# RWKV tail: outputs of the first eight heads issued between the readings of the second eight, whose banks are of the other tag

## The chip, the cores and the metric

The kernel runs on one core of one Trainium2 chip. The metric is the device time of one execution in microseconds, given as the median over several runs.

## The reference

A decoder trunk of four layers, 256 positions of width 1024, in float32. Layers 0 and 3 mix positions with RWKV-7, layer 1 with Mamba-2, layer 2 with windowed attention; each mixer stands between two half-step SwiGLU blocks, and each sub-layer is normed and shifted, scaled and gated by a vector that comes from the condition `c` through `ada_w`. The change is in the RWKV-7 mixer, and there behind the recurrence:

```
state = state * w_t + sa * (kk_t * a_t) + v_t * k_t      # per head, 64 x 64
y_t   = state @ r_t                                      # the reading
y     = (y - mean) * rsqrt(var + RW_GN_EPS) * ln_w + ln_b
bonus = sum(rh * kh * r_k) * vh
out   = ((y + bonus) * g) @ w_o
x     = x + gate * out
```

There are 16 heads of 64 channels. The sums that the norm needs run over the 64 channels of a head at each position.

## The kernel before, in words

Channels lie on the 128 partitions (two heads in a tile of 128), positions along the free axis. A tile of 128 channels and 256 positions is numbered j = 0 to 7. The 16 heads are worked in two groups g of four tiles, `jj` = 0 to 3 within the group, and the sequence in four chunks c of 64 positions.

Products with large weights take three fp32r matmuls for one in float32: weight and input are each split into a high and a low part. `unit` (L293) loads one weight tile of 512 KB on SyncE's queue into a `raw` tile, copies the high part `whi` on ScalarE (L299) and subtracts the low part `wlo` on VectorE (L303). Four `raw` tiles exist, and the modulation uses them too: `mod_step` (L247) loads one row block of `ada_w` into a `raw` tile (L252) and multiplies and sums it against `c` on VectorE (L253), with a small step behind it (L257, L261). `mod_some(n, upto)` puts n such steps into the program at that place. Of `whi` and `wlo` there are three each in the mixer.

PSUM has eight banks of 512 words, handed out by `bank(tag)` (L321): four under the tag `mm`, four under `aux`.

The program is written in one order, and a planner then sets the order of each engine's own instructions: it walks through a model of the chip's time, takes whatever is ready first, and where several are ready the one that stands earlier in the program. So an engine's order in the trace isn't the order of the source. `issue_after(ins)` forces what is traced within it behind `ins` on that engine.

Dense products can be put on a queue in pieces, each of three matmuls: `dense_queue` (L346) does so for the projections to r, k and v, and `out_proj` (L509) for the output projection, where each tile `jj` of a finished output gives eight pieces, one for each output tile of `x`, into four `mm` banks (two tiles to a bank). `fill(n)` (L370) issues the next n pieces, held behind the last product of the mixer while `hold` is set; `drain(left)` issues until `left` entries are on the queue. In the RWKV mixer `out_proj` is made with `slow=True` and `last=1`: `feed` (within it) loads the weight and puts the pieces of tile k on the queue; with the eighth tile it drains the queue, and then adds the eighth tile's products and updates `x`.

The tail of the mixer in program order, from L1552 (phase `core`):

- the chains of both groups (L1363), a step of one and a step of the other, with a `fill` and at some steps a `mod_some(1)` between. Group 0 is read within its chain by `read(0, c)` (L1402), chunk by chunk: the products go to an `mm` bank, ScalarE copies them to `ys` (L1412) and squares them (L1414), and a product with a two-column matrix of ones sums the squares into `sns`, an `mm` bank that holds 16 columns for each group.
- the last of r's queued pieces are drained.
- `bonus(4..7)` (L1336): sums on PE (L1593) into an `aux` bank, a product on VectorE (L1340), and one `mod_some(1)` each. The `fill(3)` here finds an empty queue.
- `norm(0)`, which is `rows8` (L1165): variance (L1168), reciprocal root on VectorE in 12 small steps (`rsqrt`, L573), two transposes on PE into an `aux` bank, and the split of the rows into `yth` (ScalarE, L835) and `ytl` (VectorE, L836).
- `read_heads(1, jj)` (L1419) for four tiles: the same readings for group 1, tile by tile, in an `mm` bank, with sums into the other 16 columns of `sns`, and `mod_some(2)` each.
- `outputs(0)` (L1441) for four tiles: row product `heads` (L839, products at L844) into an `aux` bank, scale and shift on VectorE (L1449, L1450), the gate's two products (`sg` and `hm`, recorded at L1077) into an `aux` bank, the gate on VectorE (L1454), the split (L318, L319), `mod_some(2)`, and `feed`.
- `norm(1)`, then `outputs(1)` in the same way; the last `feed` drains the queue.

Where a helper records the products of the mixer, all have L1077 (transposes L1081); they are told apart by their tiles. GpSimd has no part in the tail.

Of the kernel before, what the change touches and what calls it, by code (L numbers as in the profile page):

```python
# [15 lines left out]
ALU = mybir.AluOpType  # L16
# [5 lines left out]
S = 256  # L22
# [161 lines left out]
class Trunk:  # L184
# [884 lines left out]
    def rw(self, i, k):  # L1069
# [21 lines left out]
        with ExitStack() as ctx:  # L1091
# [51 lines left out]
            def lora(n, t=None):  # L1143
                return self.lora(k, n, t)
# [256 lines left out]

            def read(g, c):  # L1402

                s, uv, mr, ys, sn = ss[g], uvs[g], mrs[g], yss[g], sns[:, 16 * g : 16 * g + 16]
                o = self.bank("mm", S)
                at = slice(c * 64, c * 64 + 64)
                for jj in range(4):
                    for par, p in enumerate(half):
                        mm(hd(o, jj, p), uv[:, par, jj, c], mr[:, par, 4 * jj + c], start=True, stop=c == 0)
                    for p in half if c else ():  # L1410
                        mm(hd(o, jj, p), s[c - 1][p, jj], er[g][p, jj, c, 1:], start=False, stop=True)
                act.copy(ys[:, :, at], c64(o))  # L1412
                sq = sp.tile([P, S], F32, tag="sq", name="sq")
                act.activation(sq, o, AF.Square)  # L1414
                for jj in range(4):
                    mm(sn[half[c % 2], c // 2 * 8 + 2 * jj : c // 2 * 8 + 2 * jj + 2], sq[:, jj * 64 : jj * 64 + 64],
                       self.c("b2"), start=True, stop=True)

            def read_heads(g, jj):  # L1419

                s, uv, mr, ys, sn = ss[g], uvs[g], mrs[g], yss[g], sns[:, 16 * g : 16 * g + 16]
                o = self.bank("mm", S)
                for c in range(4):
                    at = slice(c * 64, c * 64 + 64)
                    for par, p in enumerate(half):
                        mm(o[p, at], uv[:, par, jj, c], mr[:, par, 4 * jj + c], start=True, stop=c == 0)
                    for p in half if c else ():
                        mm(o[p, at], s[c - 1][p, jj], er[g][p, jj, c, 1:], start=False, stop=True)
                act.copy(ys[:, jj], o)
                sq = sp.tile([P, S], F32, tag="sq", name="sq")  # L1430
                act.activation(sq, o, AF.Square)
                for b in range(2):
                    mm(sn[:, b * 8 + 2 * jj : b * 8 + 2 * jj + 2], sq[:, b * P : b * P + P], self.c("b2"),
                       start=True, stop=True)
# [116 lines left out]
                merge(g, *inv)  # L1551
            self.phase(f"rw{i}.core")  # L1552
            bns = slot("bn", [3, 4, P], "bn")
            sns = self.bank("mm", 32)
            hold[0] = True
            more = inner(1, bd)
            for n, _ in enumerate(one_by_one(chain(0), chain(1))):
# [4 lines left out]
                if n in (17, 20, 22):  # L1562
                    self.drain(3 - (17, 20, 22).index(n))
                    next(more)
            norm = lambda g: rows8(sns[:, 16 * g : 16 * g + 16], (ALU.mult, ALU.add), 1.0 / 64, GN_EPS)
            for jj in range(4):
                if jj >= len((17, 20, 22)):
                    self.drain(3 - jj)
                    next(more)
                self.fill(3)  # L1570
            g2, mid = lora(5), lora(4)
            for jj in range(4):
                bonus(4 + jj)
                self.mod_some(1, ahead)
                self.fill(3)
            yt = norm(0)
            yss[1] = slot("f1", [4, S], "ys")
            for jj in range(4):
                read_heads(1, jj)
                self.mod_some(2, ahead)  # L1580
                self.fill(3)
            hold[0] = False
            for _ in outputs(0, yt, g2, mid):
                pass
            for _ in outputs(1, norm(1), g2, mid):
                pass
            self.last = None

# [33 lines left out]
```

## Time and profile before

| | |
|---|---|
| median of 3 runs | 2522.41 us (2514.05 to 2526.98) |
| the profiled execution's own time | 2529.85 us |
| its span | 2527.9 us |
| granted TensorE clock, mean | 0.962 |
| TensorE busy | 2403.7 us (95%) |
| VectorE busy | 1984.8 us (79%) |
| ScalarE busy | 1262.2 us (50%) |
| tail of layer 0, from the end of the first group's sums to the last drained piece | 438.5 to 506.4 us |
| tail of layer 3, likewise | 2264.3 to 2329.9 us |

A row of the timeline gives the start in us, the duration in us, engine, line, operation, what it writes and reads, the count, and in brackets the engine's idle time ahead of it and what ended it. PE is TensorE, DVE VectorE, ACT ScalarE, SPq SyncE's DMA queue. A busy PE is not a PE at full rate: the granted clock (1.00 is full) stands in the table by stretch.

### The profile page before, as it was taken

What the parts mean: (1) busy time and instruction counts of PE and PEld (TensorE: products, weight loads), DVE (VectorE), ACT (ScalarE), POOL (GpSimd) and SP (SyncE); (2) the same over time, 40 slices, a digit from 0 to 9 for tenths busy, and PEclk for the clock granted to TensorE, in tenths of its full rate; (3) what the DMA queues carried; (4) which work ended last, traced back from release to release, by engine and by line L of the source; (5) the groups of instructions that cost most, each with busy time, mean ns of one, the idle gap of its engine ahead of it and who ended that gap; (6) DMA issues with size and microseconds to landing.
All of it is one profiled execution on the core that took longest, in us unless ns stands there. A gap on an engine that the chain in (4) does not pass through costs nothing.

```text
span 2527.9 us, 51852 instructions
## 1 busy us (share of the span) xinstructions
PE 2403.7 (95%) x20868; PEld 2247.2 (89%) x20868; DVE 1984.8 (79%) x4181; ACT 1262.2 (50%) x2261; POOL 8.1 (0%) x14
## 2 busy tenths in 40 slices
PE   6999999989999989999999999899999999998999
PEld 5998877789999988999999999799999977777999
DVE  7777687887788788988878878987788767867754
ACT  3445663254454466765445446554444465623543
POOL 0000000000000000000000000000000000000000
PEclk9999898699999999999999999989999999987999
DMA  8874224668858834455885884468758732255653
GB/s 304 288 262 167 92 94 158 234 202 291 274 196 287 285 128 135 152 178 198 302 282 188 294 286 166 151 213 293 257 180 299 263 119 72 81 174 195 211 189 117
DMA packets 145392, 521.98 MB, mean 206 GB/s; under 512 B 16128, under 2 KB 19456, under 8 KB 145024
## 3 DMA queue, kind: packets, MB, share of 16 engines
q1 hardware_dynamic: 145152, 518.67, 60.3%
q8 instruction: 164, 2.69, 0.4%
q14 instruction: 76, 0.62, 0.1%
HBM read 516.50 MB, written 2.10 MB: 205 GB/s over the span
## 4 chain that ended last, share of the span: by engine, by line
PE 52%; DMA 20%; DVE 18%; ACT 5%; issue 5%; DVEq 0%; ACTq 0%; SPq 0%
DMA raw<-ffn 11%; PE aux L1077 8%; DMA ada<-ada_w 7%; DVE wlo L303 7%; PE aux L330 5%; PE aux L328 5%; PE aux L329 5%; PE mm L328 5%; PE mm L329 4%; PE mm L330 4%; PE mm L521 3%; DVE ada L253 3%; PE mm L520 3%; PE mm L522 3%; ACT whi L299 3%
## 5 line engine op out<-in xcount | busy, mean ns | idle before, releaser
L299 ACT CAST whi<-raw 128x1024 fp32r<-128x1024 f32 x671 | 699.9, 1049 | 696.1 <-DMA raw<-ffn 476.6
L303 DVE TENSOR_TENSOR wlo<-raw,whi 128x1024 fp32r<-128x1024 f32 x671 | 816.0, 1221 | 244.0 <-ACT whi L299 240.8
L328 PE MATMUL aux<-hh,whi 128*128 128x256 f32 x2576 | 723.7, 281 | 18.6 <-DVE ft L676 16.0
L330 PE MATMUL aux<-hh,wlo 128*128 128x256 f32 x2576 | 722.1, 281 | 12.7 <-DVE wlo L303 12.4
L329 PE MATMUL aux<-hl,whi 128*128 128x256 f32 x2576 | 720.3, 280 | 0.0
L328 PEld LDWEIGHTS aux<-hh,whi 128*128 128x128 f32 x2576 | 487.7, 189 | 24.7 <-DVE ft L676 20.1
L330 PEld LDWEIGHTS aux<-hh,wlo 128*128 128x128 f32 x2576 | 488.0, 190 | 16.1 <-DVE wlo L303 16.1
L329 PEld LDWEIGHTS aux<-hl,whi 128*128 128x128 f32 x2576 | 488.2, 190 | 0.0
L253 DVE CUSTOM_DVE_ANT_0 ada<-ada,cb,vec 128x1024 f32<-128x1024 f32 x288 | 368.3, 1280 | 82.9 <-DMA ada<-ada_w 82.2
L520 PE MATMUL mm<-gh,whi 128*128 128x256 f32 x1408 | 393.4, 281 | 9.9 <-ACT gh L678 9.9
L522 PE MATMUL mm<-gh,wlo 128*128 128x256 f32 x1408 | 391.7, 281 | 3.6 <-DVE wlo L303 3.5
L521 PE MATMUL mm<-gl,whi 128*128 128x256 f32 x1408 | 393.5, 281 | 0.8 <-DVE gl L679 0.5
L328 PE MATMUL mm<-hh,whi 128*128 128x256 f32 (+1 forms) x1056 | 311.3, 301 | 13.5 <-ACT cy L885 5.1
L329 PE MATMUL mm<-hl,whi 128*128 128x256 f32 (+1 forms) x1056 | 306.3, 293 | 0.4
L330 PE MATMUL mm<-hh,wlo 128*128 128x256 f32 (+1 forms) x1056 | 305.6, 292 | 0.0
L520 PEld LDWEIGHTS mm<-gh,whi 128*128 128x128 f32 x1408 | 266.9, 190 | 11.5 <-ACT gh L678 11.5
L522 PEld LDWEIGHTS mm<-gh,wlo 128*128 128x128 f32 x1408 | 266.2, 190 | 4.9 <-DVE wlo L303 4.8
L521 PEld LDWEIGHTS mm<-gl,whi 128*128 128x128 f32 x1408 | 267.0, 190 | 2.4 <-DVE gl L679 2.4
L328 PEld LDWEIGHTS mm<-hh,whi 128*128 128x128 f32 x1056 | 203.2, 195 | 27.7 <-issue 6.8
L329 PEld LDWEIGHTS mm<-hl,whi 128*128 128x128 f32 x1056 | 205.8, 195 | 8.7 <-issue 2.3
L330 PEld LDWEIGHTS mm<-hh,wlo 128*128 128x128 f32 x1056 | 205.3, 195 | 5.9 <-issue 4.3
L678 ACT ACTIVATE gh<-ft 128x256 fp32r<-128x256 f32 x176 | 73.0, 416 | 142.2 <-DVE ft L677 141.4
(357 smaller groups left out, 2998.7 us busy)
## 6 DMA issues: line engine op xcount, KB each, us to landing
raw<-ffn SPq DMA_DIRECT2D x522, 512.0 KB, 4.6
ada<-ada_w SPq DMA_DIRECT2D x288, 512.0 KB, 4.4
raw<-rkv SPq DMA_DIRECT2D x48, 512.0 KB, 3.3
raw<-mbin SPq DMA_DIRECT2D x48, 512.0 KB, 3.3
raw<-rwo SPq DMA_DIRECT2D x16, 512.0 KB, 4.6
raw<-mbout SPq DMA_DIRECT2D x16, 512.0 KB, 3.2
lora<-lora SPq DMA_DIRECT2D x12, 512.0 KB, 3.3
raw<-qkv SPq DMA_DIRECT2D x12, 512.0 KB, 4.0
```

The lines of the kernel that those rows point to most:

```text
L253: nc.vector.tensor_tensor_reduce(out=raw, in0=raw, in1=self.cb, scale=1.0, scalar=self.v("ada_b", i * 72 + col), op0=ALU.mult, op1=ALU.add ...
L299: nc.scalar.copy(hi[:, :n], raw[:, :n])
L303: nc.vector.tensor_tensor(lo[:, :n], raw[:, :n], hi[:, :n].bitcast(F32), ALU.subtract)
L328: mm(out, hi, xh, start=start, stop=False)
L329: mm(out, hi, xl, start=False, stop=False)
L330: mm(out, lo, xh, start=False, stop=stop)
L520: mm(o, hi, xh, start=k == 0 and j % 2 == 0, stop=False, skip_group_check=True)
L521: mm(o, hi, xl, start=False, stop=False, skip_group_check=True)
L522: mm(o, lo, xh, start=False, stop=k == n - 1 and j % 2 == 1, skip_group_check=True)
L678: nc.scalar.activation(gh, t, AF.Copy, scale=0.5)
L1077: ins = nc.tensor.matmul(*a, **k)
```

## The change

Three things in `rw`, for both RWKV layers. The sums of group 0 have a bank of 16 columns for themselves (`sns`, tag `mm`), and those of group 1 a bank of their own under `aux` (`sn1`); the readings of group 1 go to `aux` banks as well. The norm of group 0 stands ahead of the bonuses in the program. And `outputs(0)` is no longer run in one go behind the readings of group 1: one step of it follows each reading, and behind it `fill(6)` issues six pieces of the output projection that `feed` has just queued.

```diff
@@ read
-                s, uv, mr, ys, sn = ss[g], uvs[g], mrs[g], yss[g], sns[:, 16 * g : 16 * g + 16]
+                s, uv, mr, ys, sn = ss[g], uvs[g], mrs[g], yss[g], sns
@@ read_heads
-            def read_heads(g, jj):
-
-                s, uv, mr, ys, sn = ss[g], uvs[g], mrs[g], yss[g], sns[:, 16 * g : 16 * g + 16]
-                o = self.bank("mm", S)
+            def read_heads(g, jj, sn):
+
+                s, uv, mr, ys = ss[g], uvs[g], mrs[g], yss[g]
+                o = self.bank("aux", S)
@@ core
-            sns = self.bank("mm", 32)
+            sns = self.bank("mm", 16)
@@ tail
-            norm = lambda g: rows8(sns[:, 16 * g : 16 * g + 16], (ALU.mult, ALU.add), 1.0 / 64, GN_EPS)
+            norm = lambda sn: rows8(sn, (ALU.mult, ALU.add), 1.0 / 64, GN_EPS)
             for jj in range(4):
                 if jj >= len((17, 20, 22)):
                     self.drain(3 - jj)
                     next(more)
                 self.fill(3)
             g2, mid = lora(5), lora(4)
+            first = outputs(0, norm(sns[:, 0:16]), g2, mid)
             for jj in range(4):
                 bonus(4 + jj)
                 self.mod_some(1, ahead)
                 self.fill(3)
-            yt = norm(0)
             yss[1] = slot("f1", [4, S], "ys")
+            sn1 = self.bank("aux", 16)
             for jj in range(4):
-                read_heads(1, jj)
+                read_heads(1, jj, sn1)
                 self.mod_some(2, ahead)
-                self.fill(3)
+                next(first)
+                self.fill(6)
             hold[0] = False
-            for _ in outputs(0, yt, g2, mid):
-                pass
-            for _ in outputs(1, norm(1), g2, mid):
+            for _ in outputs(1, norm(sn1), g2, mid):
                 pass
             self.last = None
```

## The prediction

> **What bounds the kernel now.** The page first, for the whole program.
>
> ```profile
> PE 2403.7 (95%) x20868; PEld 2247.2 (89%) x20868; DVE 1984.8 (79%) x4181; ACT 1262.2 (50%) x2261; POOL 8.1 (0%) x14
> PE 52%; DMA 20%; DVE 18%; ACT 5%; issue 5%; DVEq 0%; ACTq 0%; SPq 0%
> ```
>
> TensorE is busy 95% of the span and carries half of the chain. The change touches two stretches only, the tails of the two RWKV layers, so next comes the table by stretch for the second tail, cut where the kind of work on PE changes (columns: length, busy us and count on PE, PE's weight loads, VectorE, ScalarE and GpSimd, granted clock, DMA share, GB/s): readings, outputs of the first heads, `out_proj` pieces, the second norm, outputs of the second heads, and the last four loads of pieces.
>
> ```profile
> 2264.30:2277.00 12.70, 11.85 (x144) 8.75 (x142) 10.03 (x29) 2.64 (x8) 0.00 (x0) 1.00 0.73 244
> 2277.00:2291.70 14.70, 13.30 (x35) 8.30 (x35) 14.16 (x37) 4.71 (x7) 0.00 (x0) 0.54 0.81 263
> 2291.70:2302.00 10.30, 10.24 (x89) 10.04 (x88) 9.67 (x25) 2.51 (x3) 0.00 (x0) 1.00 0.88 294
> 2302.00:2305.80 3.80, 0.38 (x2) 0.09 (x2) 3.13 (x11) 1.31 (x2) 0.00 (x0) 0.90 0.87 320
> 2305.80:2317.10 11.30, 11.27 (x25) 6.55 (x25) 7.72 (x16) 2.26 (x4) 0.00 (x0) 0.50 0.49 173
> 2317.10:2322.20 5.10, 5.10 (x25) 5.10 (x25) 1.18 (x3) 0.41 (x1) 0.00 (x0) 0.51 0.00 0
> 2322.20:2329.90 7.70, 7.70 (x68) 7.51 (x67) 4.10 (x5) 4.16 (x7) 0.00 (x0) 1.00 0.37 132
> sum 65.60, PE 59.83 PEld 46.34 DVE 49.99 ACT 17.99 POOL 0.00; mean PE 8.55 PEld 6.62 DVE 7.14 ACT 2.57 POOL 0.00
> ```
>
> Two things set this tail. VectorE is full from 2277 to 2302 (14.16 of 14.70, 9.67 of 10.30). And PE, nearly always busy, spends three stretches at half clock (0.54, 0.50, 0.51). I keep a ledger for PE: idle 65.60 - 59.83 = 5.8 us; the cold stretches hold 13.30 + 11.27 + 5.10 = 29.7 us of work that full clock would do in half, a surcharge of 14.8 us (estimate: half of these busy times); what is left, 45.0 us, is the same work at full clock. The first tail reads alike.
>
> ```profile
> 451.40:472.00 20.60, 19.10 (x59) 13.80 (x60) 17.89 (x46) 5.62 (x9) 0.00 (x0) 0.50 0.73 253
> 482.80:494.00 11.20, 11.20 (x25) 6.49 (x25) 9.83 (x22) 2.26 (x4) 0.00 (x0) 0.50 0.54 184
> 494.00:499.40 5.40, 5.40 (x26) 5.40 (x26) 3.28 (x8) 0.07 (x1) 0.00 (x0) 0.50 0.85 272
> sum 67.90, PE 63.00 PEld 49.10 DVE 53.18 ACT 16.78 POOL 0.00; mean PE 9.00 PEld 7.01 DVE 7.60 ACT 2.40 POOL 0.00
> ```
>
> Idle 4.9, surcharge (19.10 + 11.20 + 5.40) / 2 = 17.9, work 45.1. Both tails together are 133.5 us of the program, so 0.5% (12.6 us, about what a measurement of this kernel tells from no change) needs 6.3 us out of each.
>
> **The change, part by part.** No instruction and no DMA is added or removed: the same readings, sums, outputs and pieces, in other order and other banks. So each term is idle time or clock.
>
> *The first norm, ahead of the bonuses.* This is VectorE before, its first norm (first and last step) and the start, the stop and the end of the second:
>
> ```profile
> 2267.67 0.17 DVE L1168 TENSOR_SCALAR m<-mm 128x16 f32<-128x16 f32 x1
> 2267.76 1.28 DVE L253 CUSTOM_DVE_ANT_0 ada<-ada,cb,vec 128x1024 f32<-128x1024 f32 x1
> ...
> 2276.94 0.17 DVE L1168 TENSOR_SCALAR m<-mm 128x16 f32<-128x16 f32 x1 [0.64 <-PE mm L1077]
> ...
> 2277.72 0.17 DVE L593 SCALAR_TENSOR_TENSOR ry<-rt,ry 128x16 f32<-128x16 f32 x1
> 2277.82 0.17 DVE L592 TENSOR_TENSOR rt<-rt,rh 128x16 f32<-128x16 f32 x1
> ...
> 2296.94 0.17 DVE L593 SCALAR_TENSOR_TENSOR ry<-rt,ry 128x16 f32<-128x16 f32 x1
> ...
> 2304.33 0.17 DVE L593 SCALAR_TENSOR_TENSOR ry<-rt,ry 128x16 f32<-128x16 f32 x1
> ```
>
> The norm is 13 short dependent steps (one `m`, three to start, three rounds of three). It took 2267.67 to 2277.9, 10.2 us, because the planner puts an `ada` product into the gap behind each step. Where none had landed, 2276.94 to 2277.82, about ten such steps took 0.9 us, so an undisturbed norm is about 1.3 us. And PE around it:
>
> ```profile
> 2215.05 0.31 PE L1077 MATMUL aux<-o,g 32*32 32x32 f32 x2 [1.07 <-DVE g L1304]
> 2215.29 1.11 PE L1081 MATMUL aux<-con,bk 128*128 128x128 f32 x4
> ...
> 2264.30 1.51 PE L1593 MATMUL aux<-kx,ones 64*64 64x256 f32 x10
> 2265.74 0.45 PE L1077 MATMUL mm<-mr,uv 128*64 128x64 f32 x8
> ...
> 2276.30 0.61 PE L1077 MATMUL mm<-con,sq 128*128 128x2 f32 x4 [0.76 <-ACT sq L1431]
> 2277.95 0.59 PE L1081 MATMUL aux<-con,ry 128*8 128x128 f32 x2 [1.05 <-DVE ry L593]
> 2278.99 0.58 PE L844 MATMUL aux<-yth,hot 8*128 8x256 f32 x1 [0.45 <-ACT yth L835]
> ...
> 2304.55 0.38 PE L1081 MATMUL aux<-con,ry 128*8 128x128 f32 x2 [2.61 <-DVE ry L593]
> 2305.83 0.58 PE L844 MATMUL aux<-yth,hot 8*128 8x256 f32 x1 [0.90 <-ACT yth L835]
> 2306.34 1.22 PE L1077 MATMUL aux<-sg,lora 128*128 128x256 f32 x2
> ```
>
> Before, the bonuses and the readings (2264.30 to 2276) covered the slow norm. The rows also show how banks are handed out. At 2215 PE sat idle 1.07 us for `g`, with transposes of `bk` (which need only a bank) next: they went 0.24 us behind the first product of an older `aux` tile, not before it. At 2304 PE sat idle 2.61 us with the `sg` product of the fifth output ready, and it ran only behind the norm's transpose and the row product. I read that as: banks of one tag go out in program order. After the change the transpose of the first norm comes before the four bonuses in program order, and the readings, now in `aux` too, come behind those. So the cover is gone: PE has nothing to issue (the r queue is drained) until the norm is through, and the bonuses' products and the `bonus` writes on VectorE are queued behind that. The stall is 1.3 us at least, 10.2 at most. What can cut in is what has landed by then; SyncE shows it:
>
> ```profile
> 2263.39 0.33 SPq L1034 DMA_DIRECT2D lora<-lora  x1
> 2263.82 7.09 SPq L252 DMA_DIRECT2D ada<-ada_w  x3
> 2271.87 0.33 SPq L296 DMA_DIRECT2D raw<-rwo  x1
> ...
> 2296.72 1.96 SPq L252 DMA_DIRECT2D ada<-ada_w  x2
> ```
>
> The groups of this stretch with their counts, busy time and mean in ns:
>
> ```profile
> L253 DVE CUSTOM_DVE_ANT_0 ada<-ada,cb,vec 128x1024 f32<-128x1024 f32 x16 | 20.4, 1278 | 0.3 <-DMA ada<-ada_w 0.3
> L303 DVE TENSOR_TENSOR wlo<-raw,whi 128x1024 fp32r<-128x1024 f32 x10 | 12.2, 1222 | 8.2 <-ACT whi L299 8.2
> ```
>
> Sixteen products run from 2264.3 on; three, two for each of five `rwo` loads, make 13 issued behind `lora`, so three were already on their way. In the new program order the first `rwo` load moves six `ada` loads forward on SyncE, ahead of all sixteen (the fourth stays where it is: four loads per output in place of two), so I count its split and three products: 1.3 + 1.22 + 3 x 1.28 = 6.4 us of stall. I take 6.4, nearer to the 10.2 of the same norm than to the undisturbed one. What is late next: behind the stall stand the norm's transpose, the bonuses (16 of the products of which ten took 1.51 us, 2.4 us) and the first reading (a quarter of 2265.74 to 2276.30, 2.6 us), so the first row product comes at 2264.3 + 6.4 + 0.6 + 2.4 + 2.6 = 2276 at full clock and some 5 us later at half: where it was, 2278.99, though the norm itself is done earlier.
>
> *Readings woven with outputs.* `sn1` holds one of the four `aux` banks to the second norm; reading, row product and gate product of each output share three. Behind a reading that waits for a bank stand that output's products and its pieces, and for those VectorE. Bounds: 0, and 2.3 us (the waits 0.76 + 1.05 + 0.45 above); I take 1.5, since pieces stand ready between. The freed `mm` banks gain nothing by themselves:
>
> ```profile
> 2285.59 0.41 DVE L319 TENSOR_TENSOR o<-ys,o 128x256 fp32r<-128x256 f32 x1
> 2287.89 1.22 PE L520 MATMUL mm<-o,whi 128*128 128x256 f32 x4
> ```
>
> The first piece came behind its operand, long after the sums' bank was read at 2276.94. On VectorE the work up to the fourth output is the same in sum (12 of the 16 products, four splits), and it was full there: an earlier norm cannot bring the fourth output forward by more than its idle time before 2291.7, 12.70 - 10.03 + 0.54 = 3.2 us.
>
> *The second norm.* Its wait was 3.80 - 0.38 = 3.4 us of PE idle. The fills take 24 of the first 32 pieces; 8 stay, 24 matmuls at 7.70 / 68 = 0.11 us or 2.7 us, as cover. Bounds 0 and 3.4; I take 1.0. Nothing else in it moves: its own stretching, 2296.94 to 2304.33, comes from four products that are still queued there.
>
> *Clock.* Before: 6.6 us surcharge in the first spell (13.30 / 2), 8.2 in the second ((11.27 + 5.10) / 2). After: the opening stall starts a spell too, and readings and outputs at 64 columns or in fp32 did not end one; pieces did, near 2291. I leave the first at 6.6. The second has pieces right ahead of it; bounds 0 and 8.2, I take the middle, 4.1.
>
> The Trainium skill, "TensorE: Matmul & The Clock Gate", Part 1, has the clock halve after an idle window of some 3.4 us and come back after as long a busy one. The trace halves it after gaps of 0.76, 1.05 and 0.45 us and keeps it down over 13.30 busy us, so both of its figures fail here and the rows decide; by the page's return time each spell would cost 1.7 us (an estimate), which is a rival below.
>
> Sum for one tail: 45.0 + (6.4 + 1.5 + 1.0) + (6.6 + 4.1) = 64.6 against 65.6: -1.0 us, for two tails -2. The profiled execution took 2529.85 us with a span of 2527.9 us, 7 above the median of the runs, 2522.41; no term depends on that, so 2522 - 2 = **2520 us**.
>
> **Rivals.** *Norm undisturbed* (faster): nothing lands in time or the planner keeps the steps together. Stall 1.3, and the second spell down to 2: 45.0 + 3.8 + 8.6 = 57.4, -8.2 a tail, 2506 us. For it: ten steps in 0.9 us at 2276.94. Against it: the product at 2267.76 right behind the first step. *Exposed norm, cold PE* (slower): the norm takes 10.2 us with nothing on PE, the spell behind it lasts like the first tail's (19.10 / 2 = 9.6), the second norm's idle 3.4 and spell 8.2 stay: 45.0 + 15.1 + 17.8 = 77.9, +12.3 a tail, 2547 us. It decides from idle plus surcharge above 26.9 us in a tail (now 20.6), that is from a stall of some 9 us with a second spell left whole. *VectorE holds both ends* (no change; the weave is in the program but the planner's order by readiness gives back the old one): 49.99 of 65.60 busy, full where it matters; each gain is waited away, 2522 us. *Quick clock*: each spell ends as soon as PE has been busy 3.4 us; 45.0 + 8.9 + 3.4 = 57.3, -8.3 a tail, 2506 us; 13.30 busy us at 0.54 speak against it.
>
> **How the numbers follow.** Forecast 0.42, its own range 2512 to 2530. VectorE 0.12, norm undisturbed 0.20, quick clock 0.04, exposed norm 0.22. Faster by over 0.5% (below 2509.8): most of the two fast cases and 0.05 of the forecast, 0.26. Slower (above 2535.0): 0.20 of the exposed norm and 0.04 of the forecast, 0.24. Within: 0.50. The range takes in the fast cases and the exposed norm up to two thirds of its price: 2504 to 2540.
>
> **What would show it.** A PE wait of 4 to 9 us for `ry` at the first norm's transpose, with bonuses and readings all behind it; a half-clock stretch from there; pieces between readings from about 2285; the second norm's PE wait under 2 us. Wrong if the bonuses run before that transpose (banks not in program order), if the first norm is under 2 us, or if the outputs of the second heads run at full clock throughout.

## The result, and the profile after

The change made the kernel slower: 2540.29 us median of ten runs (2525.72 to 2550.83) against 2519.51 us of the kernel before, a ratio of 1.0081 (95% interval 1.0059 to 1.0103). The forecast was 2520 us with a range of 2504 to 2540; the median lies just above that range.

The second tail of the profiled execution (2545.79 us, span 2543.7) in the same table by stretch, cut at the same changes of work: the first norm, bonuses with readings and first outputs, pieces with the last readings, the second norm, the second heads' outputs, and the last pieces.

```profile
2272.40:2281.30 8.90, 0.04 (x1) 0.01 (x1) 8.01 (x26) 1.04 (x1) 0.00 (x0) 0.68 0.95 330
2281.30:2306.30 25.00, 23.65 (x146) 16.63 (x147) 14.79 (x30) 4.08 (x10) 0.00 (x0) 0.57 0.47 161
2306.30:2321.10 14.80, 14.80 (x122) 12.46 (x121) 11.10 (x30) 3.36 (x6) 0.00 (x0) 1.00 0.64 203
2321.10:2328.30 7.20, 0.68 (x3) 0.12 (x2) 5.87 (x17) 2.45 (x3) 0.00 (x0) 0.65 0.90 313
2328.30:2339.50 11.20, 11.15 (x24) 6.48 (x24) 5.79 (x15) 1.21 (x4) 0.00 (x0) 0.50 0.25 86
2339.50:2343.90 4.40, 4.40 (x21) 4.35 (x21) 1.18 (x3) 0.41 (x1) 0.00 (x0) 0.51 0.00 0
2343.90:2352.00 8.10, 8.10 (x72) 7.91 (x70) 4.10 (x5) 4.17 (x7) 0.00 (x0) 1.00 0.36 123
sum 79.60, PE 62.81 PEld 47.96 DVE 50.84 ACT 16.72 POOL 0.00; mean PE 8.97 PEld 6.85 DVE 7.26 ACT 2.39 POOL 0.00
```

79.6 us where it was 65.6. In the prediction's ledger: idle 79.60 - 62.81 = 16.8 us (5.8 before), half-clock surcharge 23.65 x 0.43 + 11.15 x 0.50 + 4.40 x 0.49 + 0.68 x 0.35 = 18.1 (14.8), work at full clock 44.7 (45.0). The same work, with 11.0 us more idle time and 3.3 us more surcharge. The first tail went from 67.9 to 79.9 us. Both tails make +26 us; the profiled executions differ by 15.8, because the one of after is 5.9 us ahead when its first tail begins, 2 us slower between the tails and 6.3 us quicker behind the second, in parts that the change doesn't touch. How much of the 26 us every run pays a single profile doesn't show; the medians are 20.8 us apart.

PE's rows around the two norms of the second tail (timeline of the kernel after):

```profile
2271.81 0.63 PE L1077 MATMUL mm<-con,sq 128*64 128x2 f32 x8
2281.32 0.58 PE L1081 MATMUL aux<-con,ry 128*8 128x128 f32 x2 [8.88 <-DVE ry L593]
2281.83 3.68 PE L1593 MATMUL aux<-kx,ones 64*64 64x256 f32 x16
...
2327.32 0.58 PE L1081 MATMUL aux<-con,ry 128*8 128x128 f32 x2 [6.13 <-DVE ry L593]
2328.35 0.58 PE L844 MATMUL aux<-yth,hot 8*128 8x256 f32 x1 [0.45 <-ACT yth L835]
```

PE stands still for 8.88 us with the 16 bonus products ready, and they come right behind the transposes: banks do go out in program order. VectorE in that time:

```profile
2272.47 0.17 DVE L1168 TENSOR_SCALAR m<-mm 128x16 f32<-128x16 f32 x1
2272.56 1.22 DVE L303 TENSOR_TENSOR wlo<-raw,whi 128x1024 fp32r<-128x1024 f32 x1
...
2273.85 1.28 DVE L253 CUSTOM_DVE_ANT_0 ada<-ada,cb,vec 128x1024 f32<-128x1024 f32 x1
...
2277.25 1.28 DVE L253 CUSTOM_DVE_ANT_0 ada<-ada,cb,vec 128x1024 f32<-128x1024 f32 x1 [0.67 <-DMA ada<-ada_w]
...
2281.00 0.17 DVE L593 SCALAR_TENSOR_TENSOR ry<-rt,ry 128x16 f32<-128x16 f32 x1
```

One split and four products cut into the 13 steps, and at one place the engine waits for the next product's load with the norm's step queued behind it.

### The profile page after: what moved, and what is told of

Its sections match the earlier page's. It is cut to its first block, busy times and chain, and to the rows that moved or that the text cites. A ratio compares the mean times of both kernels' runs of the same rounds, so it can differ in the third digit from the quotient of the medians.

```text
span 2543.7 us, 51856 instructions
## 1 busy us (share of the span) xinstructions
PE 2397.6 (94%) x20868; PEld 2238.6 (88%) x20868; DVE 1986.9 (78%) x4181; ACT 1261.8 (50%) x2261; POOL 8.1 (0%) x14
## 4 chain that ended last, share of the span: by engine, by line
PE 54%; DMA 21%; DVE 16%; ACT 5%; issue 5%; DVEq 0%; ACTq 0%; SPq 0%
DMA raw<-ffn 11%; PE aux L1077 9%; DMA ada<-ada_w 8%; DVE wlo L303 6%; PE aux L330 5%; PE aux L328 5%; PE aux L329 5%; PE mm L328 4%; PE mm L329 4%; PE mm L330 4%; PE mm L521 4%; PE mm L520 4%; PE mm L522 4%; DVE ada L253 3%; ACT whi L299 3%
## 5 line engine op out<-in xcount | busy, mean ns | idle before, releaser
L328 PE MATMUL aux<-hh,whi 128*128 128x256 f32 x2576 | 723.1, 281 | 19.8 <-DVE ft L676 14.8
L330 PE MATMUL aux<-hh,wlo 128*128 128x256 f32 x2576 | 721.6, 280 | 12.7 <-DVE wlo L303 12.5
L328 PEld LDWEIGHTS aux<-hh,whi 128*128 128x128 f32 x2576 | 487.0, 189 | 25.7 <-DVE ft L676 18.7
L330 PEld LDWEIGHTS aux<-hh,wlo 128*128 128x128 f32 x2576 | 486.5, 189 | 16.4 <-DVE wlo L303 16.3
L253 DVE CUSTOM_DVE_ANT_0 ada<-ada,cb,vec 128x1024 f32<-128x1024 f32 x288 | 367.9, 1279 | 81.6 <-DMA ada<-ada_w 81.0
L520 PEld LDWEIGHTS mm<-gh,whi 128*128 128x128 f32 x1408 | 265.9, 189 | 10.6 <-ACT gh L678 10.5
```

The lines of the kernel that those rows point to most:

```text
L253: nc.vector.tensor_tensor_reduce(out=raw, in0=raw, in1=self.cb, scale=1.0, scalar=self.v("ada_b", i * 72 + col), op0=ALU.mult, op1=ALU.add ...
L328: mm(out, hi, xh, start=start, stop=False)
L330: mm(out, lo, xh, start=False, stop=stop)
L520: mm(o, hi, xh, start=k == 0 and j % 2 == 0, stop=False, skip_group_check=True)
```

## The experiments

All ratios are against the kernel before, run beside each kernel on the same chip; the experiments ran on five chips, so kernels of different groups are compared by ratio. The table has the ledger of both tails, made alike for all: stretches of 2 us from the end of group 0's sums to PE's wait for the first updated `x`, idle time as length less PE's busy time, and as surcharge the busy time times (1 - granted clock), an estimate good to a few us.

| kernel | ratio (95%) | median us | tails us | idle | surcharge |
|---|---|---|---|---|---|
| before | 1 | 2519.5 | 67.8, 65.6 | 4.8, 5.8 | 19.1, 14.6 |
| after | 1.0081 (1.0059 to 1.0103) | 2540.3 | 79.9, 79.6 | 17.3, 16.8 | 18.4, 18.5 |
| E1 norm behind bonuses | 1.0112 (1.0081 to 1.0142) | 2546.7 | 82.4, 80.5 | 19.2, 17.7 | 17.9, 17.0 |
| E2 banks only | 1.0104 (1.0061 to 1.0147) | 2550.5 | 82.9, 82.4 | 16.2, 15.9 | 23.5, 23.5 |
| E3 norm first only | 1.0014 (0.9989 to 1.0040) | 2527.7 | 68.7, 68.5 | 8.1, 7.3 | 16.6, 16.7 |
| E4 no pieces in the weave | 1.0103 (1.0066 to 1.0141) | 2547.6 | 81.6, 82.8 | 14.6, 15.5 | 24.2, 24.0 |
| E5 norm held together | 1.0041 (1.0021 to 1.0062) | 2532.4 | 75.8, 75.4 | 11.5, 11.0 | 18.9, 18.8 |
| E6 dense work under the norm | 1.0084 (1.0061 to 1.0107) | 2544.9 | 80.7, 79.0 | 11.7, 12.2 | 18.7, 16.4 |
| E7 second norm early | 0.9985 (0.9958 to 1.0011) | 2517.0 | 67.4, 64.3 | 8.0, 6.2 | 12.8, 11.2 |
| E8 banks, norm behind readings | 0.9995 (0.9973 to 1.0017) | 2520.0 | 68.9, 66.4 | 10.7, 8.5 | 12.7, 12.0 |
| E9 E7, held behind first norm | 0.9980 (0.9950 to 1.0009) | 2512.8 | 64.5, 60.5 | 6.4, 3.1 | 11.0, 9.6 |
| E10 E9, both norms short | 0.9971 (0.9943 to 0.9999) | 2510.2 | 65.0, 62.8 | 8.0, 4.9 | 9.1, 9.2 |
| E11 after, no products | 0.9954 (0.9922 to 0.9987) | 2510.7 | | | |
| E12 before, no products | 0.9860 (0.9817 to 0.9903) | 2485.8 | 53.9, 54.0 | 0.1, 0.1 | 8.5, 8.5 |
| E13 E2, no products | 0.9961 (0.9933 to 0.9990) | 2511.1 | 61.2, 61.2 | 3.7, 3.7 | 13.5, 13.5 |
| E14 E10, products into chains | 0.9933 (0.9905 to 0.9960) | 2504.0 | 64.2, 62.5 | 8.9, 7.0 | 9.3, 9.3 |
| E15 E14, more of them | 1.0106 (1.0072 to 1.0141) | 2547.5 | 71.7, 66.4 | 7.4, 5.3 | 20.2, 14.8 |
| E16 after, products into chains | 1.0092 (1.0064 to 1.0120) | 2544.9 | 82.9, 83.0 | 18.0, 17.0 | 19.8, 20.4 |
| E17 E14, first norm held | 0.9964 (0.9943 to 0.9985) | 2509.1 | 61.6, 57.6 | 6.1, 2.3 | 7.2, 6.8 |
| E18 E10, first norm held | 1.0029 (1.0008 to 1.0051) | 2525.2 | 73.7, 66.5 | 13.4, 10.1 | 12.8, 8.3 |

Of E11 only the time is used, since its profiled execution (2529.1 us) was the longest of its runs.

### Which of the three parts costs: E1 to E4, and E8

E1, in the kernel after:

```diff
-            first = outputs(0, norm(sns[:, 0:16]), g2, mid)
             for jj in range(4):
                 bonus(4 + jj)
                 self.mod_some(1, ahead)
                 self.fill(3)
+            first = outputs(0, norm(sns[:, 0:16]), g2, mid)
```

> The kernel after, with the first norm back behind the four bonuses; weave and banks as after. Theory 1 (exposed norm): the loss comes from the norm's transposes being handed their aux bank ahead of everything that could cover them; the 16 products of the bonuses (3.68 us at half clock, about 2.4 at full) now run ahead of them, so PE's wait for ry falls from 8.9 to some 5.5 us, and the time from 2540 by two times 3.4 to about 2533. Rival, theory 2 (the weave itself: readings, outputs and pieces in lock step on three banks): the stretches behind the first norm set the time, about 2540 (2537 to 2543).

E2, in the kernel before (readings and sums of group 1 to `aux`, nothing else):

```diff
-                s, uv, mr, ys, sn = ss[g], uvs[g], mrs[g], yss[g], sns[:, 16 * g : 16 * g + 16]
-                o = self.bank("mm", S)        # read_heads
+                s, uv, mr, ys, sn = ss[g], uvs[g], mrs[g], yss[g], sn1
+                o = self.bank("aux", S)
...
-            sns = self.bank("mm", 32)
+            sns = self.bank("mm", 16)
...
-            norm = lambda g: rows8(sns[:, 16 * g : 16 * g + 16], (ALU.mult, ALU.add), 1.0 / 64, GN_EPS)
+            norm = lambda g: rows8(sn1 if g else sns, (ALU.mult, ALU.add), 1.0 / 64, GN_EPS)
...
             yt = norm(0)
             yss[1] = slot("f1", [4, S], "ys")
+            sn1 = self.bank("aux", 16)
             for jj in range(4):
                 read_heads(1, jj)
```

> The kernel before, with one edit: the readings of the second heads and their sums go to aux banks, in the old order and without the weave. Theory 1: the readings now stand behind the first norm's transposes, which take 10 us on VectorE; the bonuses cover 2.4 to 3.7 of it, so PE waits 5 to 7 us for ry in each tail where it waited 1.05, and the time goes from 2520 to about 2531 (2528 to 2536). Theory 2: without the weave the time stays at 2520 (2517 to 2523).

E3, in the kernel before:

```diff
+            yt = norm(0)
             for jj in range(4):
                 bonus(4 + jj)
...
-            yt = norm(0)
```

> The kernel before, with one edit: the first norm ahead of the bonuses; the readings keep their mm banks, no weave. Theory 1: the bonuses now wait for the norm's bank, but the readings (10.6 us of PE in the tail before) need none of it and cover it: no new wait for ry above 2 us, time 2520 (2516 to 2524). If the place of the norm alone were the cost, whatever banks the readings have: an 8 to 9 us wait and 2535 or more. Theory 2: 2520.

E4, in the kernel after:

```diff
                 next(first)
-                self.fill(6)
```

> The kernel after without the six pieces behind each woven step (the pieces stay on the queue until the last output drains it); the rest as after. Theory 1: the first norm's 8.9 us wait stays; the pieces no longer run ahead of the last two readings, so the second norm starts earlier and has more pieces left to cover it: its wait falls from 6 to 7 us to 0 to 3.4, and the time from 2540 to about 2533 (2528 to 2538). Theory 2: pieces that push the readings back are the main cost, so nearly all of the loss goes: 2522 (2518 to 2526).

E8 is E2 with one line moved:

```diff
-            yt = norm(0)
             yss[1] = slot("f1", [4, S], "ys")
             sn1 = self.bank("aux", 16)
             for jj in range(4):
                 read_heads(1, jj)
...
+            yt = norm(0)
             hold[0] = False
```

> The kernel before, with readings and sums of the second heads in aux banks as in the run with the banks alone, but with the first norm behind the readings in the program, so that its transposes are handed their bank after theirs. Theory 1 (banks of one tag go out in program order, and that is what exposes the norm): the readings cover it again, the wait for ry is under 2 us and the time 2520 (2516 to 2526). Rival (three aux banks are too few for the readings, whatever the order): the time stays near that of the banks alone, 2540 to 2550.

E2 and E8 decide. The banks alone, without any weave, cost as much as the whole change, and a single line gives it all back: with the norm behind the readings in the program, its transposes are handed their bank after theirs. PE's rows, first of E2, then of E8 (second tail):

```profile
2264.31 1.94 PE L1594 MATMUL aux<-kx,ones 64*64 64x256 f32 x14
2276.36 0.58 PE L1081 MATMUL aux<-con,ry 128*8 128x128 f32 x2 [10.11 <-DVE ry L593]
```

```profile
2257.48 0.61 PE L1077 MATMUL aux<-con,sq 128*128 128x2 f32 x4 [0.76 <-ACT sq L1431]
...
2268.66 1.02 PE L1077 MATMUL aux<-con,sq 128*128 128x2 f32 x4 [0.76 <-ACT sq L1431]
2274.92 0.59 PE L1081 MATMUL aux<-con,ry 128*8 128x128 f32 x2 [5.24 <-DVE ry L593]
```

In E2 PE has done the bonuses and waits 10.11 us, the readings behind it. In E8 it does the four readings (their sums are the `con,sq` rows) and waits 5.24 us only then. That wait is longer than expected: VectorE runs the second norm, ready by then, in one go with the first. But PE has no second one later, and the time is that of before. So it isn't the number of `aux` banks either. E3 completes it: norm first, readings in `mm`, and only the bonuses stand behind the transposes.

```profile
2279.11 0.59 PE L1081 MATMUL aux<-con,ry 128*8 128x128 f32 x2 [4.00 <-DVE ry L593]
2279.63 3.16 PE L1593 MATMUL aux<-kx,ones 64*64 64x256 f32 x16
```

4.0 us of wait, above the 2 expected, and a time that can't be told from before. The place of the norm by itself is nearly free; what costs is that the readings stand behind it.

E1 did not come out as expected. The bonuses ran ahead, as meant, and the wait grew:

```profile
2271.35 1.94 PE L1593 MATMUL aux<-kx,ones 64*64 64x256 f32 x14
2284.77 0.59 PE L1081 MATMUL aux<-con,ry 128*8 128x128 f32 x2 [11.48 <-DVE ry L593]
```

The bonuses' four writes go ahead of the norm on VectorE, then two splits and five products cut into it: cover for PE is not gained where VectorE's queue grows as much. Nor did E4: the second norm's wait fell (4.71 us for `ry`), but the surcharge rose by 5.6 us a tail, and the time stayed.

### Is it the norm's length, or the clock: E5, E6, E16

E5, in the kernel after (the splits of the first outputs are held in the same way):

```diff
             first = outputs(0, norm(sns[:, 0:16]), g2, mid)
+            self.hold = self.last_rq        # last step of the norm
...
-                self.mod_some(1, ahead)
+                with self.tc.issue_after(self.hold):
+                    self.mod_some(1, ahead)
...
-                self.mod_some(2, ahead)
-                next(first)
+                with self.tc.issue_after(self.hold):
+                    self.mod_some(2, ahead)
+                    next(first)
```

> The kernel after, with the ada products of the bonuses and readings and the wlo splits of the first four outputs held behind the first norm's last step, so that its 13 steps run without them. Theory 1 (PE's idle time behind the exposed norm is the price): PE's wait for ry falls from 8.9 to 1.5 to 2.5 us and the time from 2540 by two times 7 to about 2526 (2520 to 2532). Rival (VectorE carries the same work either way, and what is held comes back as later outputs): the wait falls as well, but the first pieces and the second norm come no earlier, and the time stays at 2540 (2535 to 2545).

The ratio fell to 1.0041, half of the loss (the two intervals just touch), and the time to just above what theory 1 gave. Held together, the 13 steps of the first norm took 2.5 us:

```profile
2257.02 0.17 DVE L1168 TENSOR_SCALAR m<-mm 128x16 f32<-128x16 f32 x1
...
2259.32 0.18 DVE L593 SCALAR_TENSOR_TENSOR ry<-rt,ry 128x16 f32<-128x16 f32 x1
```

That is the norm undisturbed, about 0.21 us from step to step. PE's waits of E5 from 2200 to 2350 us (in total, times, longest):

```profile
PE mm L520 <- ACT whi L299: 5.7, 2, 5.4
PE aux L1081 <- DVE ry L593: 3.2, 2, 2.7
```

The wait for `ry` fell from 15.0 us in both norms to 3.2, and a new one of 5.7 us for the high part of an output weight came, which the rival had in kind: the work that was held comes back. The tail became 4.2 us shorter (79.6 to 75.4) for 11.8 us less of that wait.

E6, in the kernel after:

```diff
             first = outputs(0, norm(sns[:, 0:16]), g2, mid)
+            hot = self.bank("mm", S)
+            for q in range(48):
+                nc.tensor.matmul(hot, xh[:, q % NJ, 0:P], xl[:, q % NJ], start=q == 0, stop=q == 47)
```

> The kernel after, with 48 fp32r products of 128x256 that nobody reads, for PE to run while it waits for the first norm (5.3 us at full clock, 10.6 at half). Rival theory 3 (the cold clock behind the stall is most of the loss): PE's clock is full when the transposes come, the bonuses take 2.4 instead of 3.68 us, the 25 us at 0.57 behind the stall shrink by up to 10, and the time goes to 2520 to 2530. Theory 1 (the idle time is the price, the spell would have come anyway, as it came in the kernel before): the clock is back at half within a few us of small products, and the time stays at 2540 (2535 to 2544).

```profile
2265.18 5.57 PE L1575 MATMUL mm<-hl,hh 128*128 128x256 f32 x45
2275.39 0.58 PE L1081 MATMUL aux<-con,ry 128*8 128x128 f32 x2 [4.65 <-DVE ry L593]
2275.91 3.14 PE L1596 MATMUL aux<-kx,ones 64*64 64x256 f32 x16
```

The time is that of after. But the dense products ended 4.65 us before the transposes, and the clock had fallen by then: the bonuses took 3.14 us in place of 3.68, not 2.4. (Its idle time in the table is lower because these products count as busy.) So this run doesn't settle theory 3; the ledger does as far as it can, with 11.0 us of idle time and 3.3 of surcharge in the 14.0 us of a tail.

E16, in the kernel after: `mod_some(2, ahead)` in place of 1 at the eight places in the chains, and none with the readings.

> The kernel after with two ada steps at each place in the chains and none with the readings. Theory 1 (the exposed norm): the products that cut into it come from the bonuses and from loads on their way, and few of these go, so the wait for ry stays above 6 us and the time at 2530 to 2540. Rival (VectorE's load in the tail is what the change runs into): it falls by as much as the same edit gives elsewhere, some 8 us or more, and the wait with it.

Nothing was gained, and the waits for `ry` in the second tail are as long as ever (15.7 us in two, 15.0 in after).

### Without VectorE's products: E11 to E13

E11 and E12, in the kernel after and before; the flag is set from `lora(5)` on to the end of `rw`. E13 is the same in E2. The modulation vectors of these steps are set to one, so the three kernels don't compute the reference, and the loads of `ada_w` into `raw` tiles are gone together with the products.

```diff
         i, s, kind, j = self.todo.pop()
+        if getattr(self, "fake", 0):
+            nc.vector.memset(self.mod[i][:, s, kind, j : j + 1], 1.0)
+            return
```

> The kernel after without the ada loads and products of the tail from the bonuses on (the modulation vectors that they give are set to one, so that part is not computed). Theory 1 (the weave and the banks cost what the exposed norm costs, and that is long because products cut into it): with nothing to cut in but wlo splits the norm takes 1.3 to 3 us, PE's wait for ry falls to 1.5 to 3.5, and the time comes within 6 us of the kernel before with the same products left out. Rival (lock step of readings, outputs and pieces costs by itself): some 20 us stay between the two.

> The kernel before with the same ada loads and products left out (the modulation vectors that they give are set to one). It is the reference for the run of the kernel after without them. VectorE was full for some 25 us of each tail with 13 to 16 products of 1.28 us in it; if it sets the tail's length the time falls by 10 to 20 us to 2502 to 2512, if PE does by less than 5.

> The run with the banks alone (readings and sums of the second heads in aux banks, no weave), without the ada loads and products of the tail (the modulation vectors that they give are set to one). Beside it stand the kernel after without them (2510.7) and the kernel before without them (2485.8). Theory A (the wait behind the exposed norm, 2.7 us even without products, starts the half clock before the readings, and all small products then run at half, woven or not): 2505 to 2515. Theory B (it is the weave of readings between pieces that keeps the clock at half): with the pieces in one block the surcharge is that of the kernel before, and only the wait of some 3.5 us a tail is lost: 2493 (2489 to 2497).

The kernel before loses 34 us when these products and their loads go, more than I expected; the kernel after stays 24.9 us above it. So theory 1 as I had it then (the norm costs because products cut into it) fell: with none to cut in, the price is still there. The weave isn't the cause either, as E13 without it stands at 2511.1 us (ratio 0.9961), where E11 does (2510.7, 0.9954). The tables by stretch of the second tail, E12 and then E13, show what is left:

```profile
2243.50:2254.00 10.50, 10.50 (x138) 7.92 (x136) 4.22 (x19) 2.34 (x7) 0.00 (x0) 1.00 0.16 51
2254.00:2270.50 16.50, 16.50 (x51) 11.06 (x51) 8.04 (x28) 2.28 (x6) 0.00 (x0) 0.51 0.00 1
2270.50:2297.60 27.10, 27.01 (x199) 24.01 (x198) 15.46 (x27) 10.29 (x16) 0.00 (x0) 0.98 0.34 114
```

```profile
2246.80:2254.30 7.50, 3.95 (x47) 2.37 (x47) 4.13 (x19) 1.02 (x3) 0.00 (x0) 0.96 0.23 72
2254.30:2281.00 26.70, 26.70 (x136) 19.10 (x137) 8.05 (x28) 3.59 (x10) 0.00 (x0) 0.50 0.00 1
2281.00:2307.90 26.90, 26.79 (x202) 23.85 (x201) 15.38 (x27) 10.27 (x16) 0.00 (x0) 1.00 0.35 115
```

In E12 bonuses and readings (138 products) run at full clock ahead of the half-clock spell. In E13 PE waits 3.6 us (7.50 - 3.95) near the start, and readings and outputs (136 products) all run at half: 26.70 us in place of 16.50. The exposed norm has two prices, the wait, and that the readings, which had run warm, now run behind it. In the ledger that is 3.6 us of idle time and 5.0 of surcharge (the estimate) a tail, and a tail is 7.2 to 7.3 us longer. The two tails make 14.5 of the 16.5 us between the two profiled spans (2489.1 and 2505.6); the medians are 25 us apart, and no trace shows the difference between 16.5 and 25.

### The second norm, and a version faster than both: E7, E9, E10, E14, E15, E17, E18

E7, in the kernel before (`rows8` is split into its VectorE steps `rows8a` and the rest `rows8b`); E9 puts `issue_after(n0)` around `n1`, with `n0` the last step of the first norm; E10 puts it around the `mod_some(2, ahead)` of the readings too:

```diff
-            norm = lambda g: rows8(...)
+            norm = lambda g: rows8a(...)
...
-            yt = norm(0)
+            yt = rows8b(norm(0))
...
             hold[0] = False
+            n1 = norm(1)
             for _ in outputs(0, yt, g2, mid):
                 pass
-            for _ in outputs(1, norm(1), g2, mid):
+            for _ in outputs(1, rows8b(n1), g2, mid):
```

> The kernel before, with the 13 VectorE steps of the second norm ahead of the first heads' outputs in the program (its transposes, bank and row split stay where they were, so no bank is taken earlier). Theory 1 (a norm costs what PE has to wait for it): the rows are ready long before PE runs dry, the wait of 2.6 us goes and with it the 0.9 us for yth, and the half-clock spell behind (8.2 us surcharge a tail) shrinks by something between none and all of it: 2520 - 2 x 3.4 = 2513, down to 2497. Rival (VectorE, full from the first norm to 2302, holds the end): the steps push the outputs back by what they take, 2520 (2516 to 2524).

> The kernel before, with the second norm's 13 VectorE steps ahead of the first heads' outputs and held behind the last step of the first norm, so that the two are not mixed. Theory 1: the first norm's wait stays at 1.05 us as before and the second's 2.6 + 0.9 us goes in both tails: 2522 - 2 x 3.5 = 2515, to 2505 where the half-clock spell behind it goes as well. Rival (what the second norm gives, the outputs lose on VectorE): within 3 us of the kernel before.

> The run with the second norm early and held, with one more edit: the ada products of the readings are held behind the first norm's last step, so that fewer of them cut into it. Theory 1: the first norm is through while PE still has readings, so its 1.05 us and the 0.45 for yth go too; 2 us below the run without the hold. Rival (VectorE, full up to the fourth output, sets when the first pieces come): the first norm is shorter and the time the same as without the hold, within 3 us.

In E7 the second wait went, and the first norm, now mixed with the second, made PE wait 3.70 us in place of 1.05: no change in time. In E9 and E10 PE waits for `ry` in neither norm; 0.9980 and 0.9971 have the expected size, but only E10's interval ends below 1, barely.

E14 is E10 with `mod_some(2, ahead)` in place of 1 at the eight places in the chains and none with the readings. E15 has 3 there and none with the bonuses.

> The run with both norms short (2510.2), with two ada steps in place of one at each of the eight places in the chains and none with the readings: of the tail's 16 products some 3 go into the chains, where VectorE waits for PE by 0.3 to 3 us at a time. If VectorE sets the tail's length: 2 x 3 x 1.28 = 8 us less, 2503 (2500 to 2507). Rival (a product in the chain is as much in the way of its next step as in the tail): 2510 to 2516.

> As the run with two ada steps at each place in the chains, with three, and none with the bonuses either: some 9 products leave each tail. If VectorE sets the tail's length: up to 2 x 9 x 1.28 = 23 us less than 2510, 2490 to 2500. Rival (the chain pays for them): 2510 or more.

E14 is the fastest kernel here that computes everything: 0.9933 of before, 2504 us as expected, and so faster than both kernels; its interval overlaps that of E10, so what the move alone gives isn't shown by these two. E15 fell to the rival: the chains pay. PE waited there for a `w` (the chains' step in front of a product on PE) that stood behind three ada products on VectorE (the last 60 us of the chains ahead of the first tail):

```profile
PE aux L1077 <- DVE w L1385: 4.4, 2, 3.8
```

In the last 82 us ahead of the second tail PE was busy for 73.97 us in E15 and for 79.53 in E14. That is part of the 43.5 us between the two medians; the tails are longer too, and the rest wasn't followed.

E17 and E18 are E14 and E10 with the bonuses' four ada steps behind the first norm's last step, and the splits of the first outputs too:

```diff
-                self.mod_some(1, ahead)        # in the loop of the bonuses
...
-            n0 = self.last_rq
+            n0 = self.hold = self.last_rq
+            with self.tc.issue_after(n0):
+                self.mod_some(4, ahead)
```

> The run with two products at each place in the chains (2504.0), with the bonuses' four ada steps and the wlo splits of the first heads' outputs held behind the first norm's last step too. There PE waited 4.8 to 5.0 us for ry and 0.45 for yth in each tail, 2.79 of it for a split that stood within the norm. Theory 1: the norm is through while PE still has bonuses and readings, the wait goes, 2504 - 2 x 5.4 = 2493 (2489 to 2498). Rival (what is held comes back ahead of the first pieces): 2504 (2500 to 2508).

> The same holds without the move into the chains (from the run with both norms short, 2510.2, which has one step at each place in the chains and two with each reading). Theory 1: its waits at the first norm were already under 1 us, so only the splits come later: 2510 (2505 to 2514). If it goes as low as the run with the move and the holds, the move into the chains gives nothing by itself.

The hold left no wait for `ry` in either, and by the times neither became faster: the intervals of E17 and E14 overlap (though the tails of E17's profiled execution are 2.6 and 4.9 us shorter than those of E14's), and E18 is 0.6% (15 us) slower than E10. PE's waits of E18 from 2200 to 2350 us:

```profile
PE aux L1077 <- DVE ys L1459: 3.7, 2, 3.5
...
PE aux L844 <- DVE ys L1454: 2.3, 1, 2.3
```

The held products stand ahead of the first outputs now, and PE waits for those. Taking products out of the tail helps as far as the chains have room: E17 and E18 differ in that alone and ran beside each other, with intervals apart (0.9943 to 0.9985, 1.0008 to 1.0051). Shifting them within the tail took one wait away and brought others (E5, E18).

## Why the prediction was wrong, point by point

The sum was 64.6 us for a tail; the second one took 79.6. (Both tails are 30 us above the forecast, the median 20.)

| term | forecast | bounds | measured | off by |
|---|---|---|---|---|
| opening stall | 6.4 | 1.3 to 10.2 | 8.9 | +2.5 |
| woven bank waits | 1.5 | 0 to 2.3 | 1.35 (25.00 - 23.65) | -0.15 |
| second norm's idle | 1.0 | 0 to 3.4 | 6.5 (7.20 - 0.68) | +5.5 |
| first cold spell | 6.6 | kept | 10.2 (23.65 x 0.43) | +3.6 |
| second cold spell | 4.1 | 0 to 8.2 | 7.7 | +3.6 |

- *Banks in program order*: right, and the root of the loss. The row at 2281.83 shows it, and E2 against E8 by time.
- *The opening stall*: right in kind and within its bounds, too small. I counted one split and three products; there were four, and VectorE waited 0.67 us for one of them. My 1.3 us for the undisturbed norm was a misreading as well: the ten steps in 0.9 us at 2276.94 belong to two norms that alternate, and E5 has 2.5 us for one alone. That would have made the sum's stall 7.6.
- *The first row product where it was*: it came 16.2 us behind the start of the tail (2288.64), against 14.7 before; near enough.
- *"An earlier norm cannot bring the fourth output forward", VectorE being full*: it was put back instead. Its split came at 2317.78, 45.4 us into the tail, against 2296.61, 32.3 us. VectorE was no longer the one that is full; it waited 13.9 us for row products where it had waited 2.0:

```profile
L1449 DVE SCALAR_TENSOR_TENSOR ys<-ys,vec,aux 128x256 f32<-128x256 f32 x8 | 3.8, 480 | 13.9 <-PE aux L844 13.9
```

- *The second norm's idle*: the failed step. I took 1.0 us, let left-over pieces cover 2.7 us of the norm and said that nothing else in it moves; 6.5 us were measured. The cover held (pieces ran beside it up to 2321.19, 4.7 us), but the norm moved. Its sums came behind the last reading, so all 13 steps were still to do, with four products and two splits of weights among them: 10.5 us, from the first of the rows below to the last. Before, the sums came ahead of the first heads' outputs, six steps were done by 2278, and only the other seven took the 7.4 us from 2296.94 to 2304.33. The bound of 3.4 us from before didn't hold, since it was the bound of a norm that had started earlier.

```profile
2316.49 0.17 DVE L1168 TENSOR_SCALAR m<-aux 128x16 f32<-128x16 f32 x1
...
2327.00 0.17 DVE L593 SCALAR_TENSOR_TENSOR ry<-rt,ry 128x16 f32<-128x16 f32 x1
```

- *The clock*: the first spell was not kept at its 6.6 us; I had said that the opening stall starts a spell, and left the price as it was without a reason. The readings and bonuses, at full clock before in this tail, now run behind the stall (23.65 us busy at 0.57). The second spell wasn't halved; pieces right ahead of it did nothing for it.
- *The rivals*: "exposed norm, cold PE" gave 77.9 us a tail and 2547 us; 79.9, 79.6 and 2540.3 were measured, and its point of decision, a stall of some 9 us with a second spell left whole, is what the trace shows. It had a chance of 0.22. That its sum is so close is partly luck: its stall was 1.3 us too long and its second norm's idle 3.1 too short. I had no evidence against it, only my choice of values within the bounds: the stall's bound of 10.2 us came from the very same norm, with the same products on their way. "VectorE holds both ends" failed, as its 50.84 of 79.60 us show.

Of what was to show it, the wait for `ry`, the half clock and the pieces from 2285 on (2298.26 in fact) were looked for in the right places; the second norm's wait under 2 us was the sign that failed, and outputs of the second heads at half clock belong to the rival.

## What to carry to other kernels

Where a bank is handed out in program order, a tile whose operand is late holds up every later tile of that tag, ready or not; so before work is moved to other banks or up in the program, list what stands behind it in that tag and ask what covers the wait. A short dependent chain on a busy engine takes as long as the long operations that fill its gaps make it (2.5 us became 8.7 to 10.5 here), and holding these back takes that wait away and brings others, so ask which stretch has room for them. Of terms with bounds, those that rest on the same rows go to the same end together; taken each near its middle or below they added up to no change here, and all at their slow end to the rival that came close.

## What the runs showed of the hardware

In these traces the clock follows a wait and dense work within some 3 to 5 us, and is also lost among small products without such a wait. The granted clock by microsecond in the second tail of the kernel after:

```profile
2275.00:2276.00 1.00, 0.00 (x0) 0.00 (x0) 1.00 (x4) 0.00 (x0) 0.00 (x0) 0.77 1.04 393
...
2285.00:2286.00 1.00, 1.00 (x14) 0.49 (x10) 0.73 (x4) 0.00 (x0) 0.00 (x0) 0.61 0.79 246
2286.00:2287.00 1.00, 1.00 (x18) 0.74 (x16) 1.00 (x2) 0.00 (x0) 0.00 (x0) 1.00 0.93 344
...
2289.00:2290.00 1.00, 1.00 (x4) 0.41 (x2) 0.82 (x2) 0.48 (x1) 0.00 (x0) 0.60 0.93 340
```

PE's last sums ended at 2272.4: the clock halved some 3 us later, was back some 4.5 us after work began at 2281.32, and halved again at 2289, where the longest gap was 0.76 us (2288.11). In E12 it fell near 2254 with PE busy for 10.50 of 10.50 us before, and in the first tail of the kernel before at 448.2, among readings, with PE busy without a gap from 438.5 on. Where the clock changes there is a grid: placed by the share of half clock in stretches of 0.5 us (an estimate), the changes come at 2275.54, 2285.78, 2289.19, 2306.26, 2323.33 and 2343.81 here, and at 2277.76, 2291.42, 2305.07 and 2322.14 in the kernel before, always a whole number of 3.41 us apart (3, 1, 5, 5 and 6; 4, 4 and 5). So a half-clock spell grows or shrinks by steps of 3.41 us, each worth an estimated 1.7 us of surcharge (half of 3.41) where PE is busy throughout; what in a step decides, these traces don't show. The Trainium skill, "TensorE: Matmul & The Clock Gate", Part 1, has the clock fall after an idle window of some 3.4 us and come back after as long a busy one. The first fall and the return agree with it, and so does the end of the spell of before (pieces from 2287.89 on, full clock near 2291); my prediction rejected both figures too flatly (of the three gaps that it named, the one of 0.45 us came behind the fall at 2277.76). The falls at 2289 and in E12, with no such window, don't agree, and nor does the spell of before, where the small products of the outputs, busy for nine microseconds, didn't bring the clock back.

Equal work at the same granted clock took different times in two executions: the last 191 to 198 us of the program, 1608 matmuls in each, kept PE busy for 191.17 us in the kernel before and 184.81 in the kernel after, though the change doesn't touch that part and the granted clock reads 1.00 in nearly all of it (0.92 in the first 20 us of both). The sums by stretch, before and after:

```profile
sum 198.00, PE 191.17 PEld 190.34 DVE 124.61 ACT 91.41 POOL 0.00; mean PE 38.23 PEld 38.07 DVE 24.92 ACT 18.28 POOL 0.00
```

```profile
sum 191.70, PE 184.81 PEld 184.00 DVE 124.65 ACT 91.55 POOL 0.00; mean PE 36.96 PEld 36.80 DVE 24.93 ACT 18.31 POOL 0.00
```

What sets that is open; it is a reason to compare medians of many runs, and tails within a profile, before whole spans.
